# An encoder layer on one core: v's products ordered by the arrival of their weights, part of q moved behind v(1), block sums in x's old places, and some loads and splits issued sooner

## Chip, cores, metric

The kernel runs on one core of one Trainium2 chip. The metric is the device time of one execution in microseconds (us). The engines are called as in the profile: PE or TensorE (products), PEld (its weight loads), DVE or VectorE, ACT or ScalarE, POOL or GpSimd, SP (the queue that issues nearly all transfers).

## What is computed

One encoder layer on 1024 tokens of width 1024, in float32:

```python
h = layer_norm(x, emb_ln_g, emb_ln_b)
proj = h @ w_in                      # columns: q k v z_attn (512 each), u z_lru (512 each), g_attn g_lru (1024 each)
attn = neighbourhood_attention(q, k, v, rpb)       # 8 heads of 64, window 8 x 16 on a 16 x 64 grid
y_a  = attn * silu(z_a)
u    = centred_depthwise_conv(u, conv_w, conv_b)
y_b  = (rg_lru(u, ..., forward) + rg_lru(u, ..., backward)) * silu(z_b)
m    = sigmoid(g_a + b_merge[0]) * (y_a @ w_ba) + sigmoid(g_b + b_merge[1]) * (y_b @ w_bb)
out  = layer_norm(ALPHA * h + m @ w_out, ln_g, ln_b)
```

## The kernel before

The 1024 tokens are eight tiles of 128, i = 0 to 7. Every float32 operand of a product is split into a high and a low half that TensorE takes at full rate (ScalarE or POOL rounds the high half, `lo_of` subtracts it for the low one), and a product of two such operands is three products: high by high, low by high, high by low (`mm3`, the product at L131).

All five engines run in the order in which the code is written (`manual_schedule`), so an instruction that waits holds up what stands behind it in its engine's queue. The places in SBUF and PSUM are shared by tags; a tile waits for the last reader of what was there before.

The stages, in order:

- **Tiles, v and q** (lines 370 to 590). `load_x(i)` fetches a tile of x into one of five places (tag x). `ln_sums` takes mean and variance, `ln_v` (VectorE, tiles 0, 1, 3) or `ln_scale` and `ln_g` (ScalarE and POOL, the others) normalize it in place, `keep(i)` stores it for the end of the layer. `turn(i, kk)` transposes it on TensorE into a PSUM bank, four blocks of 128 columns in each half kk; `turn_hi` (ScalarE, L263) and `turn_lo` (VectorE) make the halves b_h and b_l of it. wv comes in four loads (`load_wv`) and is split by `wv_hi` (ScalarE, L186) and `wv_lo` (POOL). `v_part(i, kind, ks)` issues v's products of tile i (L308) for the weight blocks ks: kind h is b_h by wv's high half, a is b_l by the high half, w is b_h by the low half; 8 blocks each, 24 products in all. `q_part(m, n)` does the same for 128 columns m of q and k (m = 0 to 3) and 512 tokens n, with weights loaded by `qk_load` and split by `qk_prep` (ScalarE L169, POOL). The gains and offsets of the first layer norm are spread over the partitions by TensorE into four banks (gps) and copied to SBUF by `gb_copy`.
- **Block sums.** For tiles 4 to 7, `t_full` and `t_last` (L281 to L290) form sums of blocks of the transposed tile that the next stage multiplies, and `t_hi` and `t_lo` split them. t2 is written by `t_full` and overwritten by `t_last`.
- **Block stage.** 16 pairs of output columns, each by seven products of blocks (a11, a12, s2, s1, s3, s4, a22) in a loop over slots, for k, z, u and the gates; convolution and RG-LRU (`gate_stage`) run in the same slots. At slot `HEAD_AT` (109) and after it the first head's q, bias and k are fetched (`load_head`: `load_q`, `load_k`), and in `ending(2)` the second head's.
- **Attention.** Per head and tile: scores (L1036), bias and row minimum (L1046), exp (L1051), transposes (L1058), products with v (L1082). The merge of the LRU branch fills TensorE between them.
- **Late merge** (a loop over slots from L1253). `b_group` multiplies y_a with wb, `merge` applies the gate, adds the other branch and splits the sum; `b_split(0, j, A)` splits the weights of column block j, ScalarE the high half (L840), POOL the low one (L125). Of wb two blocks are held at a time.
- **Output** projection and layer norm, tile by tile; the last tile in pieces of 256 columns.

[...]

The order of the first products before the change:

```python
    for k in K0:
        v_part(0, "h", (k,))
        v_part(0, "a", (k,))
    v_part(0, "w", K0)
    v_part(0, "h", K1)
    v_part(0, "a", K1)
```

Of the kernel before, what the change touches and what calls it, by code (L numbers as in the profile page):

```python
# [67 lines left out]
def encoder_kernel(ctx, tc, x, gb1, gb, w_qk, w_v, w_s, w_ba, w_bb, w_gate, smalls, bias, w_out, out):  # L68
# [96 lines left out]

    def qk_prep(m):
        st = qk_s.pop(m)
        hi, lo = qk_w[m] = pair(wpl, [P, NK, P], f"wqk{m}", tag="w", bufs=2)
        A.copy(hi[:], st[:])  # L169
        lo_of(G, lo[:], st[:], hi[:])  # L170
# [3 lines left out]
    def load_x(i):  # L174
        xs[i] = ln.tile([P, D], F32, tag="x", bufs=5, name=f"x{i}")
        if i == 0:
            for c in range(2):
                SP.dma_start(xs[i][:, halves[c]], x[i][:, halves[c]])
        else:
            SP.dma_start(xs[i][:], x[i])  # L180
# [26 lines left out]
    def ln_sums(i):  # L207
        st, mv, e = (ln.tile([P, n], F32, tag=f"ln{n}{c}", bufs=2, name=f"ln{i}{c}")
                     for n, c in ((12, "t"), (2, "m"), (4, "e")))
        sts[i] = st, mv, e[:, 3:4], e[:, 0:3]  # L210
        sd, ve = sts[i][2:]
        for c in range(2):
            V.bn_stats(st[:, 6 * c:6 * c + 6], xs[i][:, halves[c]])
        V.bn_aggr(mv[:], st[:].rearrange("p (c s) -> p c s", c=2))
        A.activation(sd, mv[:, 1:2], AF.Sqrt, bias=eps_t[:])
        V.tensor_scalar(ve[:, 0:1], mv[:, 1:2], EPS, -0.5, ALU.add, ALU.mult)
# [59 lines left out]
    def t_full(i):  # L276

        for c, tag in ((1, "a21"), (2, "a12"), (3, "a22")):
            tt[i, c] = wsp.tile([P, 4, P], F32, tag=tag, bufs=2 if c == 3 else 1, name=f"t{c}_{i}")
        t1, t2, t3 = (tt[i, c][:] for c in (1, 2, 3))  # L280
# [6 lines left out]
    def t_last(i):  # L287
        t2 = tt[i, 4] = tt[i, 2]
        V.tensor_tensor(t2[:], f(B21[0], i), t2[:], ALU.subtract)
        V.tensor_tensor(t2[:], t2[:], f(B21[1], i), ALU.add)  # L290

    def t_hi(i, *cs):
        for c in cs:
            A.copy(Ts[c][0][:, :, ti(i)], tt[i, c][:])

    def t_lo(i, *cs):
        for c in cs:
            lo_of(G, Ts[c][1][:, :, ti(i)], tt[i, c][:], Ts[c][0][:, :, ti(i)])
# [28 lines left out]
    def q_part(m, n):  # L327
        o = qos[m, n] = bank(f"q{m}_{n}")
        run(mm3(o[:], [([t[:, 4 * kk + k, :] for t in qk_w[m]], [t[:, k, :] for t in blocks[kk][n]])
                       for kk in range(2) for k in range(4)]))  # L330
# [48 lines left out]
    load_wv(2)  # L379
    load_x(2)  # L380
    load_wv(3)
    SP.dma_start(sm[:], smalls)
    load_x(3)
    qk_load(0)
    load_x(4)
# [23 lines left out]
    turn_lo(0, 0)  # L409
    ln_sums(1)  # L410
    turn_lo(0, 1)
    for k in range(4, 8):
        wv_hi(k)
    for k in KS:
        wv_lo(k)
    for k in K0:
        v_part(0, "h", (k,))
        v_part(0, "a", (k,))
    v_part(0, "w", K0)
    v_part(0, "h", K1)  # L420
# [3 lines left out]
    keep(1)  # L424
    load_x(6)
    for kk in BOTH:
        turn(1, kk)
        turn_hi(1, kk)
    ln_sums(2)
    for z in BOTH:  # L430
        gb_copy(z, 0)
    ln_scale(2)
    for kk in BOTH:
        turn_lo(1, kk)
    for z in BOTH:
        gb_copy(z, 1)
    ln_g(2)
    ln_sums(3)
    v_part(1, "h", KS)
    v_part(0, "w", K1)  # L440
    v_part(1, "a", KS)
    qk_prep(0)
    v_hi(0)
    ln_v(3, 0)
    ln_v(3, 1)
    ln_sums(4)
    v_lo(0)
    psg.release()
    pst = tc.alloc_tile_pool(name="pst0", bufs=4, space=bass.MemoryType.PSUM, reuse_waits="tile")
    banks[0] = pst  # L450
# [4 lines left out]
    def tile_in(i, between=None, *args):  # L455

        for kk in BOTH:
            banks[0] = pst
            turn(i, kk)
            turn_hi(i, kk)  # L460
            banks[0] = ps0
            if kk == 0 and between:
                between(*args)
# [10 lines left out]
    banks[0] = ps0  # L474
    keep(2)
    keep(3)
    v_store(0)
    tile_in(2, v_part, 1, "w", KS)
    tile_in(3)
    tile_lo(2)  # L480
    ln_scale(4)
    ln_g(4)
    v_hi(1)
    tile_lo(3)
    qk_load(1)
# [4 lines left out]
    v_part(2, "h", KS)  # L490
    v_part(2, "a", KS)
    v_part(2, "w", KS)
    qk_prep(1)
# [3 lines left out]
    v_part(3, "h", KS)  # L497
    v_part(3, "w", KS)
# [6 lines left out]
    ln_next(7)  # L505
    t_full(4)
    v_part(3, "a", KS)
    t_hi(4, 2, 1, 3)
# [4 lines left out]
    q_part(0, 0)  # L513
    t_lo(4, 2, 1, 3)
    tile_in(5)
    q_hi(0, 0)
    tile_lo(5)
    t_last(4)
    q_lo(0, 0)
    q_store(0, 0)  # L520
    t_hi(4, 4)
    t_lo(4, 4)
# [6 lines left out]
    t_hi(5, 2, 1, 3)  # L529
    t_lo(5, 2, 1, 3)  # L530
    tile_in(6)
    tile_lo(6)
    t_last(5)
    t_hi(5, 4)
    t_lo(5, 4)
    for kind in "hwa":
        v_part(4, kind, KS)
    v_hi(4)
    v_lo(4)
    v_store(4)  # L540
    for kind in "hwa":
        v_part(5, kind, KS)
    tile_in(7)
    tile_lo(7)
    t_full(6)
    t_hi(6, 2, 1, 3)
    t_lo(6, 2, 1, 3)
    v_hi(5)
# [4 lines left out]
    t_lo(6, 4)  # L553
    for kind in "hwa":
        v_part(6, kind, KS)
    t_full(7)
    v_hi(6)
    v_lo(6)
# [336 lines left out]
    at(HEAD_AT, 1, lambda: load_k(0))  # L895
    at(HEAD_AT - 3, 1, head_start)
# [61 lines left out]
    def ending(k):  # L958
# [5 lines left out]
        if k == 2:  # L964
# [3 lines left out]
            load_head(1)  # L968
# [284 lines left out]
    for slot in range(2 * NK + 2):  # L1253
# [11 lines left out]
        if j < NK:  # L1265
# [179 lines left out]
```

## Time and profile before

| | |
|---|---|
| time, median of 3 runs | 683.49 us (683.47 to 684.93) |
| the profiled execution | 684.63 us, its span 682.8 us |
| granted TensorE clock, mean | 0.997 |
| TensorE busy | 665.8 us, 98% |
| VectorE, ScalarE, POOL busy | 72%, 53%, 52% |
| moved by DMA | 113.40 MB, mean 166 GB/s |

A row of the timeline is: start in us from the span's start, duration in us, engine, line of the kernel, operation, output <- inputs, shape, count, and in brackets the engine's idle time before it with what ended it. Rows that follow each other without a pause are merged (xN). A matmul's row ends with a modelled tail, so that rows overlap. SPq is SP's queue of issues. In the list of waits the numbers are: us in total, how often, the longest. Names are cut of their numbers: wv is v's weights, b_h and b_l the transposed tile's halves, ht the split block sums, tp a transpose in PSUM, ks and qs a head's k and q, wb the merge's weights, wo those of the output.

### The profile page before, as it was taken

Reading aid. Unit: us, or ns where it says so; the run is one execution under the profiler, and the core shown is the slowest. Engines: PE = TensorE matmul, PEld = TensorE weight load, DVE = VectorE, ACT = ScalarE, POOL = GpSimd, SP = SyncE. Lnnn points to the kernel's source line nnn. Section 1 sums busy time; section 2 is a strip of 40 time slices with the busy share of each in tenths; the row PEclk is TensorE's granted clock in tenths of the full one; section 3 lists DMA queues with packets and bytes.
Section 4 is the critical chain, followed back from the end, with each engine's and each line's share of the span. In section 5 each row is a group of like instructions: output and inputs, shape, how many; then the busy total and the mean of one; then the engine's idle time right before and its main releaser. Section 6 shows DMA issues by size and latency. Waiting matters only on the chain.

```text
span 682.8 us, 9299 instructions
## 1 busy us (share of the span) xinstructions
PE 665.8 (98%) x3177; PEld 554.4 (81%) x3177; DVE 494.7 (72%) x821; ACT 363.9 (53%) x612; POOL 353.8 (52%) x258
## 2 busy tenths in 40 slices
PE   7999999999999999999999999999999999999995
PEld 6787888888888888888788888788888878888884
DVE  7866766796899599879977785378787777533434
ACT  4544524247686677768576634467777554310110
POOL 5697461444576577567647544115355446435442
PEclk9999999999999999999999999999999999999998
DMA  8654165223324233431453557898794457512211
GB/s 327 227 187 154 63 231 171 78 92 124 124 92 145 71 108 123 170 124 48 170 199 112 182 176 253 305 353 308 250 327 144 176 197 271 189 62 93 92 62 61
DMA packets 48703, 113.40 MB, mean 166 GB/s; under 512 B 5057, under 2 KB 9745, under 8 KB 47121
## 3 DMA queue, kind: packets, MB, share of 16 engines
q1 hardware_dynamic: 48624, 112.81, 47.4%
q8 instruction: 25, 0.41, 0.2%
q14 instruction: 22, 0.17, 0.1%
q10 hardware_dynamic: 32, 0.01, 0.0%
HBM read 77.11 MB, written 35.68 MB: 165 GB/s over the span
## 4 chain that ended last, share of the span: by engine, by line
PE 80%; DVE 8%; DMA 4%; POOL 3%; issue 2%; ACT 1%; SPq 1%; DVEq 0%; POOLq 0%; ACTq 0%
PE a L131 29%; PE o L131 13%; PE s L131 11%; PE mb L131 10%; PE q L131 5%; PE acc L1082 3%; PE pt L1058 3%; PE s L1036 3%; POOL x L243 2%; PE v L308 2%; PE g L734 2%; DMA wvsl<-in_w_v_dram 1%; DMA ks<-k_d 1%; DMA wb<-in_w_ba_dram 1%; DVE ws_l L125 1%
## 5 line engine op out<-in xcount | busy, mean ns | idle before, releaser
L131 PE MATMUL o<-wo_h,ml 128*128 128x512 f32 (+1 forms) x136 | 51.2, 377 | 0.0
L131 PE MATMUL o<-wo_l,mh 128*128 128x512 f32 (+1 forms) x136 | 51.2, 376 | 0.0
L131 PE MATMUL o<-wo_h,mh 128*128 128x512 f32 (+1 forms) x136 | 51.2, 376 | 0.0
L1046 DVE CUSTOM_DVE_ANT_0 sc<-s,bias 128x384 f32<-128x384 f32 (+1 forms) x64 | 33.5, 523 | 22.9 <-PE s L1036 14.0
L131 PE MATMUL a<-ht_h,ws_h 128*128 128x512 f32 x128 | 49.9, 390 | 0.0
L131 PE MATMUL a<-ht_h,ws_l 128*128 128x512 f32 x128 | 49.8, 389 | 0.0
L131 PE MATMUL a<-ht_l,ws_h 128*128 128x512 f32 x128 | 49.8, 389 | 0.0
L131 PE MATMUL a<-b_h,wa_h 128*128 128x512 f32 x128 | 49.8, 389 | 0.0
L131 PE MATMUL a<-b_h,wa_l 128*128 128x512 f32 x128 | 49.8, 389 | 0.0
L131 PE MATMUL a<-b_l,wa_h 128*128 128x512 f32 x128 | 49.8, 389 | 0.0
L1335 DVE SCALAR_TENSOR_TENSOR z<-z,o 128x512 f32<-128x512 f32 (+1 forms) x17 | 11.2, 656 | 51.0 <-PE o L131 51.0
L1066 ACT CAST pt_h<-pt 128x384 fp32r<-128x384 f32 x64 | 29.0, 453 | 26.4 <-PE pt L1058 18.3
L1345 POOL TENSOR_TENSOR z<-z,gb 128x1024 f32<-128x1024 f32 x7 | 16.8, 2395 | 48.5 <-ACT z L1344 48.5
L1051 ACT ACTIVATE p<-sc,summ 128x384 f32<-128x384 f32 (+1 forms) x64 | 37.9, 592 | 5.2 <-DVE summ L1046 5.0
L1314 ACT ACTIVATE sd<-mv,eps_z 128x1 f32<-128x1 f32 x8 | 2.4, 294 | 67.1 <-DVE mv L1340 67.1
L308 PE MATMUL v<-wv,b_h 128*128 128x512 f32 x128 | 32.8, 399 | 2.7 <-ACT b_h L263 1.6
L125 DVE TENSOR_TENSOR pt_l<-pt,pt_h 128x384 fp32r<-128x384 f32 x64 | 33.2, 519 | 2.1 <-ACT pt_h L1066 1.6
L1036 PE MATMUL s<-ks,qs 128*128 128x384 f32 (+1 forms) x128 | 31.3, 326 | 1.1 <-DMA ks<-k_d 1.1
L308 PEld LDWEIGHTS v<-wv,b_h 128*128 128x128 f32 x128 | 23.6, 188 | 9.3 <-ACT b_h L263 2.3
L842 POOL CAST wb_h<-wb 128x512 fp32r<-128x512 f32 x9 | 7.0, 777 | 46.1 <-PE s L1036 18.3
L125 POOL TENSOR_TENSOR wb_l<-wb,wb_h 128x512 fp32r<-128x512 f32 x16 | 22.0, 1374 | 16.1 <-ACT wb_h L840 15.4
L1058 PEld LDWEIGHTS pt<-ident,p 128*128 128x128 f32 x176 | 23.1, 140 | 8.5
(438 smaller groups left out, 2199.8 us busy)
## 6 DMA issues: line engine op xcount, KB each, us to landing
ks<-k_d SPq DMA_DIRECT2D x8, 1024.0 KB, 8.0
h_d<-x SPq DMA_DIRECT2D x8, 512.0 KB, 4.4
v_d<-vs SPq DMA_DIRECT2D x8, 512.0 KB, 3.7
q_d<-q SPq DMA_DIRECT2D x8, 512.0 KB, 3.0
ga_d<-ga SPq DMA_DIRECT2D x16, 256.0 KB, 2.0
gb_d<-gb SPq DMA_DIRECT2D x16, 256.0 KB, 2.0
k_d<-k SPq DMA_DIRECT2D x8, 512.0 KB, 4.0
qs<-q_d SPq DMA_DIRECT2D x8, 512.0 KB, 3.9
```

Of the source, the lines that this page charges most:

```text
L125: eng.tensor_tensor(lo, full, hi.bitcast(F32), ALU.subtract)
L131: PE.matmul(o, a, b, start=first and i == 0, stop=last and i == len(prods) - 1, skip_group_check=not (first and last))
L243: G.tensor_tensor(z[:, halves[c]], z[:, halves[c]], gb_t[w][c][:], op)
L308: PE.matmul(vos[i][:], a, wv[kind == "w"][k][:], start=vn[i] == 0, stop=vn[i] == 23)
L734: PE.matmul(o[:, n, :], w[:, 2 * d + b, :], us[b][:, n * HALF:(n + 1) * HALF], start=z == 0, stop=z == 1)
L1036: PE.matmul(o[:, :P * len(near(t))], q[:, t * P:(t + 1) * P], k[:, z, keys], start=z == 0, stop=z == 1)
L1046: V.tensor_tensor_reduce(s[:, :w], o[:, :w], heads[h][2][:, b0:b0 + w], -1.0, 3.0e38, ALU.add, ALU.min, accum_out=sums[h][0][:, t:t + 1])
L1051: A.activation(probs[h % 2][t][:], scs.pop((h, t))[:, :w], AF.Exp, bias=sums[h][0][:, t:t + 1], scale=-1.0, accum_out=sums[h][1][:, t:t + 1])
L1058: PE.transpose(tp[:, n * P:(n + 1) * P], probs[h % 2][t][:, z * P:(z + 1) * P], ident[:])
L1066: A.copy(pt[0][:, span(b)], tps[h, b][:, :P * len(near(b))])
L1082: PE.matmul(acc[g][:, d:d + w], vvs[h // 2][:, b, h % 2, :], pt[:, a:a + w], start=b in (1, 6) and z == 0, stop=z == 1 and b == (4, 7)[g])
L1345: G.tensor_tensor(z[:], z[:], gb2[:, 0, :], ALU.mult)
```

## The change

Edits, in the order of the kernel:

- In the first stage the four banks of `ps0` get fixed places in a written order instead of the next free one.
- The loads: wv(3) goes ahead of x(2), wqk0 ahead of x(3), the small parameters behind x(4); wqk1 is issued ahead of x(6).
- The gains' copies are spread; wqk0's split stands right behind wv's, ahead of tile 1's b_h, and wqk1's ahead of tile 2's.
- v(0)'s products come as w0 w1, h4 h5, w2 w3, h6 h7 and so on; v(1) starts on the first half of tile 1. q(0,0) is issued in two parts of 256 tokens, the first behind v(1), the second behind v(3). The transposes of tiles 2 and 3 come in halves, those of tiles 6 and 7 one v earlier.
- The block sums t1, t2 and t4 take places of x that are free by then; t4 no longer overwrites t2.
- The second head's q, bias and k are issued right behind the first head's k.
- In the late merge, at slots 1 and 2, the split of the next weights stands ahead of the merge.

```diff
...
     hb12 = pool("hb12", "right")
 
     turns = []
+    places = itertools.chain((0, 1, 2, 3, 0, 1, 2, 0, 2, 3, 1), itertools.cycle((2, 3, 0, 1)))
 
     def bank(name):
         if turns:
             return banks[0].tile([P, HALF], F32, tag=next(turns[0]), bufs=2, name=name)
+        if banks[0] is ps0:
+            return ps0.tile([P, HALF], F32, tag=f"b{next(places)}", bufs=1, name=name)
         return banks[0].tile([P, HALF], F32, tag="bank", name=name)
...
         qk_s[m] = wpl.tile([P, NK, P], F32, tag="ws", bufs=1, name=f"wqk{m}_s")
         SP.dma_start(qk_s[m][:], w_qk[m])
 
+    def qk_hi(m):
+        qk_w[m] = pair(wpl, [P, NK, P], f"wqk{m}", tag="w", bufs=2)
+        A.copy(qk_w[m][0][:], qk_s[m][:])
+
+    def qk_lo(m):
+        hi, lo = qk_w[m]
+        lo_of(G, lo[:], qk_s.pop(m)[:], hi[:])
+
     def qk_prep(m):
-        st = qk_s.pop(m)
-        hi, lo = qk_w[m] = pair(wpl, [P, NK, P], f"wqk{m}", tag="w", bufs=2)
-        A.copy(hi[:], st[:])
-        lo_of(G, lo[:], st[:], hi[:])
+        qk_hi(m)
+        qk_lo(m)
 
     xs, sts = {}, {}
...
         xs[i] = ln.tile([P, D], F32, tag="x", bufs=5, name=f"x{i}")
         if i == 0:
-            for c in range(2):
-                SP.dma_start(xs[i][:, halves[c]], x[i][:, halves[c]])
+            for sl in halves:
+                SP.dma_start(xs[i][:, sl], x[i][:, sl])
         else:
...
     def gb_copy(z, c):
         A.copy(gb_t[z][c][:], gps[z][c][:])
 
-    def ln_sums(i):
+    def ln_stats(i):
         st, mv, e = (ln.tile([P, n], F32, tag=f"ln{n}{c}", bufs=2, name=f"ln{i}{c}")
...
         for c in range(2):
             V.bn_stats(st[:, 6 * c:6 * c + 6], xs[i][:, halves[c]])
         V.bn_aggr(mv[:], st[:].rearrange("p (c s) -> p c s", c=2))
+        V.tensor_scalar(ve[:, 0:1], mv[:, 1:2], EPS, -0.5, ALU.add, ALU.mult)
+
+    def ln_root(i):
+        st, mv, sd, ve = sts[i]
         A.activation(sd, mv[:, 1:2], AF.Sqrt, bias=eps_t[:])
-        V.tensor_scalar(ve[:, 0:1], mv[:, 1:2], EPS, -0.5, ALU.add, ALU.mult)
+
+    def ln_sums(i):
+        ln_stats(i)
+        ln_root(i)
 
...
 
     def t_full(i):
 
-        for c, tag in ((1, "a21"), (2, "a12"), (3, "a22")):
-            tt[i, c] = wsp.tile([P, 4, P], F32, tag=tag, bufs=2 if c == 3 else 1, name=f"t{c}_{i}")
-        t1, t2, t3 = (tt[i, c][:] for c in (1, 2, 3))
+        tt[i, 3] = wsp.tile([P, 4, P], F32, tag="a22", bufs=2, name=f"t3_{i}")[:]
+        t12 = ln.tile([P, 2, 4, P], F32, tag="x", bufs=5, name=f"t12_{i}")
+        tt[i, 1], tt[i, 2] = t12[:, 0], t12[:, 1]
+        if i in (4, 6):
+            tt["last"] = ln.tile([P, 2, 4, P], F32, tag="x", bufs=5, name=f"t4_{i}")
+        tt[i, 4] = tt["last"][:, i % 2]
+        t1, t2, t3 = (tt[i, c] for c in (1, 2, 3))
         A.copy(t3, tp4(i, 0))
...
         V.tensor_tensor(t3, tp4(i, 1), t3, ALU.subtract)
 
     def t_last(i):
-        t2 = tt[i, 4] = tt[i, 2]
-        V.tensor_tensor(t2[:], f(B21[0], i), t2[:], ALU.subtract)
-        V.tensor_tensor(t2[:], t2[:], f(B21[1], i), ALU.add)
+        t4 = tt[i, 4]
+        V.tensor_tensor(t4, f(B21[0], i), tt[i, 2], ALU.subtract)
+        V.tensor_tensor(t4, t4, f(B21[1], i), ALU.add)
 
     def t_hi(i, *cs):
         for c in cs:
-            A.copy(Ts[c][0][:, :, ti(i)], tt[i, c][:])
+            A.copy(Ts[c][0][:, :, ti(i)], tt[i, c])
 
     def t_lo(i, *cs):
         for c in cs:
-            lo_of(G, Ts[c][1][:, :, ti(i)], tt[i, c][:], Ts[c][0][:, :, ti(i)])
+            lo_of(G, Ts[c][1][:, :, ti(i)], tt[i, c], Ts[c][0][:, :, ti(i)])
 
...
 
     qos = {}
 
-    def q_part(m, n):
-        o = qos[m, n] = bank(f"q{m}_{n}")
-        run(mm3(o[:], [([t[:, 4 * kk + k, :] for t in qk_w[m]], [t[:, k, :] for t in blocks[kk][n]])
-                       for kk in range(2) for k in range(4)]))
+    def q_part(m, n, cols=slice(0, HALF)):
+        if (m, n) not in qos:
+            qos[m, n] = bank(f"q{m}_{n}")
+        run(mm3(qos[m, n][:, cols], [([t[:, 4 * kk + k, :] for t in qk_w[m]], [t[:, k, cols] for t in blocks[kk][n]])
+                                     for kk in range(2) for k in range(4)]))
 
...
     load_wv(1)
     load_x(1)
     load_wv(2)
+    load_wv(3)
     load_x(2)
-    load_wv(3)
+    qk_load(0)
+    load_x(3)
+    load_x(4)
     SP.dma_start(sm[:], smalls)
-    load_x(3)
-    qk_load(0)
-    load_x(4)
 
...
     wv_hi(3)
     turn_hi(0, 1)
     turn_lo(0, 0)
+    gb_copy(0, 0)
+    wv_hi(4)
+    wv_hi(5)
     ln_sums(1)
     turn_lo(0, 1)
-    for k in range(4, 8):
-        wv_hi(k)
+    wv_hi(6)
+    wv_hi(7)
+    gb_copy(1, 0)
     for k in KS:
         wv_lo(k)
+    qk_prep(0)
     for k in K0:
         v_part(0, "h", (k,))
         v_part(0, "a", (k,))
-    v_part(0, "w", K0)
-    v_part(0, "h", K1)
+    v_part(0, "w", (0, 1))
+    v_part(0, "h", (4, 5))
+    v_part(0, "w", (2, 3))
+    v_part(0, "h", (6, 7))
     v_part(0, "a", K1)
     ln_v(1, 0)
     ln_v(1, 1)
     keep(1)
+    qk_load(1)
     load_x(6)
-    for kk in BOTH:
-        turn(1, kk)
-        turn_hi(1, kk)
-    ln_sums(2)
-    for z in BOTH:
-        gb_copy(z, 0)
-    ln_scale(2)
-    for kk in BOTH:
-        turn_lo(1, kk)
+    turn(1, 0)
+    turn_hi(1, 0)
+    v_part(0, "w", (4, 5))
+    v_part(1, "h", K0)
+    turn(1, 1)
     for z in BOTH:
         gb_copy(z, 1)
+    turn_hi(1, 1)
+    v_part(0, "w", (6, 7))
+    ln_stats(2)
+    turn_lo(1, 0)
+    ln_root(2)
+    v_hi(0)
+    ln_scale(2)
+    turn_lo(1, 1)
     ln_g(2)
+    v_part(1, "w", K0)
+    v_part(1, "h", K1)
+    v_part(1, "a", KS)
+    v_part(1, "w", K1)
     ln_sums(3)
-    v_part(1, "h", KS)
-    v_part(0, "w", K1)
-    v_part(1, "a", KS)
-    qk_prep(0)
-    v_hi(0)
+    q_part(0, 0, slice(0, 256))
     ln_v(3, 0)
     ln_v(3, 1)
-    ln_sums(4)
-    v_lo(0)
+    v_hi(1)
+    qk_prep(1)
     psg.release()
     pst = tc.alloc_tile_pool(name="pst0", bufs=4, space=bass.MemoryType.PSUM, reuse_waits="tile")
-    banks[0] = pst
     for c, pl in zip((4, 3, 1, 2), hts):
         Ts[c] = pair(pl, [P, 4, HALF], f"ht{c}", tag=f"ht{c}")
     T1, T2, T3, T4 = (Ts[c] for c in (1, 2, 3, 4))
 
-    def tile_in(i, between=None, *args):
-
+    def turned_in(i, kk):
+        banks[0] = pst
+        turn(i, kk)
+        turn_hi(i, kk)
+        banks[0] = ps0
+
+    def tile_in(i):
         for kk in BOTH:
-            banks[0] = pst
-            turn(i, kk)
-            turn_hi(i, kk)
-            banks[0] = ps0
-            if kk == 0 and between:
-                between(*args)
+            turned_in(i, kk)
 
...
         ln_scale(i)
         ln_g(i)
 
-    banks[0] = ps0
     keep(2)
     keep(3)
+    turned_in(2, 0)
+    turned_in(3, 0)
+    ln_sums(4)
+    v_lo(0)
     v_store(0)
-    tile_in(2, v_part, 1, "w", KS)
-    tile_in(3)
-    tile_lo(2)
+    turned_in(2, 1)
+    turned_in(3, 1)
     ln_scale(4)
     ln_g(4)
-    v_hi(1)
+    tile_lo(2)
     tile_lo(3)
-    qk_load(1)
     v_lo(1)
     v_store(1)
     load_x(7)
     ln_next(5)
-    v_part(2, "h", KS)
-    v_part(2, "a", KS)
-    v_part(2, "w", KS)
-    qk_prep(1)
+    for kind in "hwa":
+        v_part(2, kind, KS)
     keep(4)
     ln_next(6)
     v_hi(2)
-    v_part(3, "h", KS)
-    v_part(3, "w", KS)
+    for kind in "hw":
+        v_part(3, kind, KS)
     v_lo(2)
...
     tile_in(4)
     tile_lo(4)
     ln_next(7)
+    v_part(3, "a", KS)
     t_full(4)
-    v_part(3, "a", KS)
-    t_hi(4, 2, 1, 3)
     v_hi(3)
     v_lo(3)
     v_store(3)
     keep(6)
-    q_part(0, 0)
-    t_lo(4, 2, 1, 3)
+    q_part(0, 0, slice(256, HALF))
+    t_last(4)
     tile_in(5)
     q_hi(0, 0)
+    t_hi(4, 2, 1, 3, 4)
+    t_lo(4, 2, 1, 3, 4)
     tile_lo(5)
-    t_last(4)
     q_lo(0, 0)
     q_store(0, 0)
-    t_hi(4, 4)
-    t_lo(4, 4)
     keep(7)
     q_part(1, 0)
...
     q_lo(1, 0)
     q_store(1, 0)
-    t_hi(5, 2, 1, 3)
-    t_lo(5, 2, 1, 3)
-    tile_in(6)
-    tile_lo(6)
     t_last(5)
-    t_hi(5, 4)
-    t_lo(5, 4)
     for kind in "hwa":
         v_part(4, kind, KS)
+    tile_in(6)
     v_hi(4)
+    t_hi(5, 2, 1, 3, 4)
+    t_lo(5, 2, 1, 3, 4)
+    tile_lo(6)
     v_lo(4)
     v_store(4)
+    t_full(6)
     for kind in "hwa":
         v_part(5, kind, KS)
     tile_in(7)
-    tile_lo(7)
-    t_full(6)
+    v_hi(5)
     t_hi(6, 2, 1, 3)
     t_lo(6, 2, 1, 3)
-    v_hi(5)
+    tile_lo(7)
     v_lo(5)
     v_store(5)
...
     t_hi(6, 4)
     t_lo(6, 4)
+    t_full(7)
     for kind in "hwa":
         v_part(6, kind, KS)
-    t_full(7)
     v_hi(6)
+    t_last(7)
     v_lo(6)
...
                 qk_prep(m + 2)
                 if m == 0:
                     qk_load(3)
-                    t_hi(7, 2, 1, 3)
-                    t_lo(7, 2, 1, 3)
-                    t_last(7)
-                    t_hi(7, 4)
-                    t_lo(7, 4)
+                    t_hi(7, 2, 1, 3, 4)
+                    t_lo(7, 2, 1, 3, 4)
                     s_load(0, "a21", "a22", "a12")
...
         at(slot + 3, 0, lambda t=t: yb_lo(t))
     at(HEAD_AT, 1, head_pool)
     at(HEAD_AT, 1, lambda: load_k(0))
+    at(HEAD_AT, 1, lambda: load_head(1))
     at(HEAD_AT - 3, 1, head_start)
...
             b_load(1, 2)
             for n in range(2):
                 g_load(1, 1, n)
-            load_head(1)
         if k < 2:
...
             run(b_group(0, j, n, ya, o, range(3 if slot < 2 else 4)))
             if 0 < slot < 3:
                 run(b_group(0, 0, slot - 1, ya, sums_m[slot - 1], range(3, 4)))
-                merge(0, slot - 1, sums_m[slot - 1])
             if n == 0 and j > 0:
                 b_split(0, j + 1, A)
+            if 0 < slot < 3:
+                merge(0, slot - 1, sums_m[slot - 1])
```

## Prediction

> **What bounds the kernel now.** I read the page's head, then TensorE's own list of waits, then TensorE's timeline, and last the other engines around each hole.
>
> ```profile
> span 682.8 us, 9299 instructions
> PE 665.8 (98%) x3177; PEld 554.4 (81%) x3177; DVE 494.7 (72%) x821; ACT 363.9 (53%) x612; POOL 353.8 (52%) x258
> PE v L308 <- ACT b_h L263: 1.6, 3, 0.9
> PE s L1036 <- DMA ks<-k_d: 1.1, 1, 1.1
> PE mb L131 <- POOL wb_l L125: 0.9, 1, 0.9
> PE mb L131 <- ACT wb_h L840: 0.5, 1, 0.5
> ```
>
> TensorE is busy for 98% of the span, so the change can't lift the bound; it can only close holes. The list names three places: v's first products, the second head's keys, and the weights (wb) of the last merge. The change touches all three.
>
> **Before 38 us.** First a ledger of TensorE from v's first product to tile 4's transposes:
>
> ```profile
> 9.88 0.50 PE L308 MATMUL v<-wv,b_h 128*128 128x512 f32 x1
> 28.70 2.11 PE L308 MATMUL v<-wv,b_h 128*128 128x512 f32 x8 [0.49 <-ACT b_h L263]
> 32.46 5.61 PE L308 MATMUL v<-wv,b_h 128*128 128x512 f32 x24
> 37.90 1.03 PE L254 MATMUL tp<-ident,x 128*128 128x128 f32 x8
> 38.69 2.10 PE L308 MATMUL v<-wv,b_l 128*128 128x512 f32 x8
> ```
>
> 24 products take 37.90 - 32.46 = 5.44 us, 0.227 each; 8 transposes take 38.69 - 37.90 = 0.79. Between 9.88 and 37.90 lie 28.0 us with 88 products (20.0; v(0) to v(2) and two thirds of v(3)) and 24 transposes (2.4): 5.6 us are holes, nearly all before 28.7.
>
> The change moves wv(3)'s load ahead of x(2)'s, orders v(0)'s products by the arrival of weights, lets v(1) begin on half a tile, splits wqk0 behind the last of wv, and issues q(0,0) for its first 256 tokens behind v(1): 24 half-width products. Their price stands in the last tile of the output projection, where 24 steps lie between these two starts:
>
> ```profile
> 671.72 0.28 PE L131 MATMUL o<-wo_l,mh 128*128 128x256 f32 x1
> 674.60 0.28 PE L131 MATMUL o<-wo_l,mh 128*128 128x256 f32 x1
> ```
>
> That is 2.88 us, 0.120 each. Half of a full-width pass costs 2.72, so the split adds 0.16 per half. Whether the half fits the holes is decided by those who supply TensorE:
>
> ```profile
> 8.91 5.02 POOL L125 TENSOR_TENSOR wv<-wvsh,wv 128x512 fp32r<-128x512 f32 x4 [7.60 <-ACT wv L186]
> 13.88 5.01 POOL L125 TENSOR_TENSOR wv<-wvsl,wv 128x512 fp32r<-128x512 f32 x4
> 10.78 1.29 DVE L213 BATCH_NORM_STATS2 ln1t<-x 128x6 f32<-128x512 f32 x2 [0.23 <-DMA x<-in_x_dram]
> 14.65 1.14 ACT L186 CAST wv<-wvsl 128x512 fp32r<-128x512 f32 x2 [0.98 <-DMA wvsl<-in_w_v_dram]
> 14.42 0.75 DVE L230 SCALAR_TENSOR_TENSOR x<-x,ln1e,gps 128x512 f32<-128x512 f32 x1
> 17.75 1.07 ACT L263 CAST b_h<-tp 128x512 fp32r<-128x512 f32 x2 [1.95 <-PE tp L254]
> 22.89 1.03 ACT L169 CAST wqk_h<-wqk_s 128x1024 fp32r<-128x1024 f32 x1
> 21.37 5.25 POOL L243 TENSOR_TENSOR x<-x,gb 128x512 f32<-128x512 f32 x4 [2.48 <-ACT x L237]
> 26.59 2.35 POOL L125 TENSOR_TENSOR wqk_l<-wqk_s,wqk_h 128x1024 fp32r<-128x1024 f32 x1
> ```
>
> POOL makes one low half of wv each 1.25 us, the last at 18.9, in either order. From x(1)'s landing (10.78) to wv(3)'s (14.65) three loads of 512 KB arrive, 1.29 each. In the new order wv(3) lands near 13.4, x(2) near 14.7, wqk0 near 15.9.
>
> Walked through, in the new order: h4 and h5 fill the time until w3's low half is made (13.9); v(0)'s a products end at 15.7; tile 1's first transposes follow at once, its first half being ready at 14.42 + 0.75 = 15.2. Now ScalarE is late: wqk0's cast (15.9 to 16.9) stands in its queue ahead of tile 1's b_h (0.54, to 17.5), and behind that wait v(1) h and VectorE's b_l. After w4, w5 (to 16.65) TensorE waits 0.9. w6, w7 and v(1) then run to 23.9, q's half to 26.8. Tile 2's square root now stands behind tile 1's second b_h on ScalarE, so POOL starts x(2)'s gains at 22.35 instead of 21.37 and ends them at 27.6: a hole of 0.5 before x(2)'s second half is turned. wqk1's load goes out when POOL frees its place (18.9 + 2.35 = 21.3), lands behind x(5) and h(1) near 26.5, and its cast delays b_h of tiles 2 and 3: a hole of 0.2 in v(2) h. POOL does wqk1's low part between tiles 2 and 4, so tile 4 is ready near 36.7. I arrive at tile 4's transposes at 37.85, where it was 37.90, with half of q(0,0) done: a gain of 2.7. Bounds: 1.0 if wqk0 and wqk1 land one load (1.3) late less what holes remain behind them; 4.2 if the 0.9, 0.5 and 0.2 close too.
>
> At no cost: wqk1's issue ahead of x(6), which waits for h(1)'s store anyway; the gains' copies, two of 0.5 put into ScalarE's wait for wv (0.98 in the row at 14.65). If that wait is gone they cost 0.5.
>
> **38 to 77 us.**
>
> ```profile
> 64.19 1.19 PE L254 MATMUL tp<-ident,x 128*128 128x128 f32 x8
> 66.24 3.96 PE L308 MATMUL v<-wv,b_h 128*128 128x512 f32 x16 [0.86 <-ACT b_h L263]
> 47.83 0.69 DVE L282 TENSOR_TENSOR t<-tp,b_h 128x512 f32<-128x512 f32 x1 [1.83 <-ACT t L281]
> 48.56 0.93 DVE L283 TENSOR_TENSOR t<-t,b_l 128x512 f32<-128x512 f32 x1
> 50.13 0.68 DVE L285 TENSOR_TENSOR t<-tp,t 128x512 f32<-128x512 f32 x1
> 52.42 0.69 DVE L125 TENSOR_TENSOR vs<-v,vs 128x512 fp32r<-128x512 f32 x1 [1.61 <-ACT vs L315]
> 53.03 1.28 DVE L125 TENSOR_TENSOR b_l<-tp,b_h 128x512 fp32r<-128x512 f32 x2
> 57.16 1.77 DVE L289 TENSOR_TENSOR t<-b_h,t 128x512 f32<-128x512 f32 x1 [2.85 <-POOL ht_l L125]
> 58.96 1.66 DVE L290 TENSOR_TENSOR t<-t,b_l 128x512 f32<-128x512 f32 x1
> 69.09 0.69 DVE L290 TENSOR_TENSOR t<-t,b_l 128x512 f32<-128x512 f32 x1
> ```
>
> Before, v(6) starts 2.05 after tile 7's transposes, which need 0.79; ScalarE's queue is late with b_h. Now tiles 6 and 7 are turned one v ahead, which leaves b_h 5.4 us. Gain 1.2, less 0.16 for q's second half (the first's is inside the 2.7). With t4 in a place of its own L289 no longer waits 2.85 for POOL.
>
> Late next is VectorE's chain. From 47.83: t_full(4) 3.0, v's low 0.7, t_last(4) 3.4, b_l(5) 1.3, q's low 0.7, t_full(5) 3.0, q's low 0.7, t_last(5) 2.4 (between the two lengths of L290), b_l(6) 1.3, end 64.3. TensorE wants b_l(6) at 37.85 + transposes of four tiles 3.2, v(3) a 1.8, q's half 2.9, then q(1,0), v(4), v(5) 16.3, and 16 products of v(6) 3.6: 65.7. Slack 1.4, no stall in the sum; bounds 0 and 2.
>
> L290 takes 0.69 in one row and 1.66, beside a POOL pass, in another. [...]
>
> **Second head.**
>
> ```profile
> 422.37 0.55 SPq L864 DMA_DIRECT2D ks<-k_d  x1
> 434.73 1.87 SPq L864 DMA_DIRECT2D ks<-k_d  x1
> 443.65 0.47 PE L1036 MATMUL s<-ks,qs 128*128 128x256 f32 x2 [1.07 <-DMA ks<-k_d]
> ```
>
> Head 1's keys went out 12.4 us after head 0's and landed 1.07 too late; now they go right behind them, near 424. Gain 1.1. Its 2 MB now stand in SP's queue ahead of the last gates' stores and the next merge's first loads (g, wb), at 1.29 per 512 KB some 5 us. g(1,0,0) then lands about a microsecond after VectorE wants it, which nobody on TensorE waits for. Bounds: 0 (landing no sooner) and 1.2.
>
> **Late merge.**
>
> ```profile
> 550.11 1.05 ACT L1280 CAST wo_h<-wos 128x1024 fp32r<-128x1024 f32 x1
> 552.79 0.62 ACT L840 CAST wb_h<-wb 128x512 fp32r<-128x512 f32 x1
> 553.46 0.50 PE L131 MATMUL mb<-ya_h,wb_h 128*128 128x512 f32 x1 [0.50 <-ACT wb_h L840]
> 553.49 1.28 POOL L125 TENSOR_TENSOR wb_l<-wb,wb_h 128x512 fp32r<-128x512 f32 x1 [7.76 <-ACT wb_h L840]
> 554.82 0.50 PE L131 MATMUL mb<-ya_h,wb_l 128*128 128x512 f32 x1 [0.86 <-POOL wb_l L125]
> ```
>
> The holes are 0.5 with a busy tail of 0.16, and 1.36 - 0.23 = 1.13 between the two products: 1.8. wb_h waited in ScalarE's queue behind the merge's cast. Put ahead of it, it starts at 551.2, wb_l ends near 553.2; TensorE wants wb_h at 552.8, wb_l at 553.0. Gain 1.5 (bounds 0.8, with POOL's pass held up by VectorE, and 1.8). The merge's own cast waits for VectorE, not for ScalarE.
>
> **Sum.** 2.7 + 1.2 - 0.16 + 1.1 + 1.5 = 6.3, and 0.05 from 37.90 to 37.85: 6.4. The profiled execution took 684.63 (1.8 around its span of 682.8) and would take 678.2; the runs' median, 683.49, goes to **677.1**. A measurement of this kernel can't tell less than 0.2% (1.4 us) from no change. The forecast's own range is 675.7 (1.4 of the holes left before 38 us closed) to 678.6 (1.5 of the 6.4 lost).
>
> **Rivals.**
> A. The hole moves to ScalarE: wqk0's and wqk1's casts wait for their transfers with b_h behind them. For it: the 0.9 already in my walk. Against: 1.29 per load is steady. Price 1.8, a load and a half: 678.9. Chance 0.15.
> B. VectorE's chain sets v(6) and v(7): t3 has one place until v(7) is done, so its copy on ScalarE waits for POOL, with b_h(7) behind it. For it: a slack of 1.4 only. Price 2, the bound above: 679.1. Chance 0.12.
> C. Head 1's loads help nothing, since SP or the transfers are full: 1.1 lost, 678.2. Chance 0.06.
> A and B together, with their stalls doubled, come within 0.2% (over 682.1): chance 0.03.
> [...] Chance 0.06, other mishaps included.
>
> **How the numbers follow.** The forecast has 0.58, A 0.15, B 0.12, C 0.06: faster 0.91; same 0.03; slower 0.06. The range 675.5 to 680.2 holds the forecast, C, and most of A and B; it leaves out A with B, D, and the case that all bounds are reached (4.2 + 1.2 - 0.16 + 1.2 + 1.8 = 8.2, 675.3).
>
> **What would show it.** Right: tile 4's transposes near 37.9 behind 24 half-width q products; no wait before v(6); the first product after v(7) near 73.4; no ks wait on TensorE; wb waits under 0.4. Wrong: v(1) h later than 18.5 with wqk0's cast in front (A); v(6) or v(7) released by b_h or b_l (B, D); keys still landing after the first scores of head 1 (C).

## The result, and the profile after

The changed kernel takes 678.42 us (median of six runs, 677.68 to 678.67); the kernel before, beside it, 683.48 (683.09 to 684.93). The ratio of the means is 0.9919 [0.9906, 0.9931] (in brackets, here and below, the 95% interval). The forecast was 677.1, range 675.5 to 680.2. The profiled execution took 678.46 us, its span 676.7; 678.2 was forecast for it. In the runs beside the experiments the kernel before took 684.5 to 684.7 and the changed one 678.88, a ratio of 0.9911 [0.9898, 0.9924].

The head of the page of after, and two rows of its list of TensorE's waits:

```profile
span 676.7 us, 9344 instructions
PE 665.2 (98%) x3201; PEld 555.7 (82%) x3201; DVE 492.7 (73%) x821; ACT 364.5 (54%) x612; POOL 355.8 (53%) x258
PE v L328 <- ACT b_h L279: 0.5, 1, 0.5
PE mb L134 <- DVE ya_l L128: 0.3, 1, 0.3
```

TensorE's busy time hardly moved (665.8, now 665.2); of the 6.1 us that the span lost, 5.5 came out of its holes. The waits for the second head's keys and for wb are gone from the list. In before v waited three times for b_h and once each for POOL's wv, ScalarE's wv and b_l; now it waits once, for b_h.

The timeline of after up to tile 4's transposes, ScalarE's and POOL's rows first, then TensorE's:

```profile
15.37 1.05 ACT L171 CAST wqk_h<-wqk_s 128x1024 fp32r<-128x1024 f32 x1 [0.93 <-DMA wqk_s<-in_w_qk_dram]
16.32 0.58 ACT L279 CAST b_h<-tp 128x512 fp32r<-128x512 f32 x1
21.76 5.29 POOL L259 TENSOR_TENSOR x<-x,gb 128x512 f32<-128x512 f32 x4 [2.15 <-ACT x L253]
16.95 1.19 PE L328 MATMUL v<-wv,b_h 128*128 128x512 f32 x4 [0.53 <-ACT b_h L279]
17.98 0.60 PE L270 MATMUL tp<-ident,x 128*128 128x128 f32 x4
26.32 1.91 PE L270 MATMUL tp<-ident,x 128*128 128x128 f32 x16
27.98 3.96 PE L328 MATMUL v<-wv,b_h 128*128 128x512 f32 x16
37.23 1.03 PE L270 MATMUL tp<-ident,x 128*128 128x128 f32 x8
```

The order of the walk is seen: wqk0's cast waits for its transfer, tile 1's b_h stands behind it, v(1) h waits for that, at 16.95. POOL's gains end at 27.05, and no hole stands ahead of the 16 transposes of tiles 2 and 3, since q's half runs until 26.3. Tile 4's transposes start at 37.23 (37.85 forecast).

From tile 5 to v(7) in after, TensorE, VectorE, ScalarE:

```profile
61.00 1.03 PE L270 MATMUL tp<-ident,x 128*128 128x128 f32 x8
61.79 3.89 PE L328 MATMUL v<-wv,b_h 128*128 128x512 f32 x16
65.51 1.98 PE L328 MATMUL v<-wv,b_l 128*128 128x512 f32 x8
47.07 1.79 DVE L303 TENSOR_TENSOR t<-t,b_l 128x512 f32<-128x512 f32 x1
57.83 0.69 DVE L302 TENSOR_TENSOR t<-tp,b_h 128x512 f32<-128x512 f32 x1 [2.51 <-ACT t L301]
58.55 0.69 DVE L303 TENSOR_TENSOR t<-t,b_l 128x512 f32<-128x512 f32 x1
61.08 1.45 DVE L309 TENSOR_TENSOR t<-b_h,t 128x512 f32<-128x512 f32 x1
62.56 1.67 DVE L310 TENSOR_TENSOR t<-t,b_l 128x512 f32<-128x512 f32 x1
64.15 1.27 DVE L128 TENSOR_TENSOR b_l<-tp,b_h 128x512 fp32r<-128x512 f32 x2
57.21 0.59 ACT L301 COPY t<-tp 128x512 f32<-128x512 f32 x1 [3.03 <-POOL ht_l L128]
```

v(6) follows the transposes at once, and the first product after v(7) starts at 72.77 (73.4 forecast). But tile 6's two low halves end at 64.15 + 1.27 = 65.42, and TensorE takes the first of them at 65.51: 0.1 us between, where the forecast had 1.4.

In the last merge of after, and POOL's gate in before (the last row):

```profile
546.61 0.62 ACT L865 CAST wb_h<-wb 128x512 fp32r<-128x512 f32 x1
547.31 1.30 POOL L128 TENSOR_TENSOR wb_l<-wb,wb_h 128x512 fp32r<-128x512 f32 x1 [6.03 <-ACT wb_h L865]
541.88 0.50 PE L134 MATMUL mb<-ya_l,wb_h 128*128 128x512 f32 x1 [0.31 <-DVE ya_l L128]
537.04 2.54 POOL L1145 TENSOR_TENSOR za<-za,rsb 128x512 f32<-128x512 f32 x2 [9.54 <-DMA rsb<-rs_d]
541.47 2.54 POOL L1120 TENSOR_TENSOR za<-za,rsb 128x512 f32<-128x512 f32 x2 [8.68 <-DMA rsb<-rs_d]
```

The waits for wb are gone. This profile has a short one for ya_l in their place, which follows the last row sums (rsb) on their way back from memory: POOL's gate starts 0.52 after the merge's first product (536.52), in before (541.47) 0.27 ahead of it (541.74). Counted from start to start, 0.23 is lost ahead of ya_h and 0.48 ahead of ya_l.

### The profile page after: what moved, and what is told of

Its sections match the earlier page's. It is cut to its first block, busy times and chain, and to the rows that moved or that the text cites. A ratio compares the mean times of both kernels' runs of the same rounds, so it can differ in the third digit from the quotient of the medians.

```text
span 676.7 us, 9344 instructions
## 1 busy us (share of the span) xinstructions
PE 665.2 (98%) x3201; PEld 555.7 (82%) x3201; DVE 492.7 (73%) x821; ACT 364.5 (54%) x612; POOL 355.8 (53%) x258
## 4 chain that ended last, share of the span: by engine, by line
PE 89%; DVE 6%; DMA 2%; issue 1%; SPq 1%; ACT 0%; POOL 0%; DVEq 0%; POOLq 0%
PE a L134 30%; PE o L134 13%; PE mb L134 12%; PE s L134 11%; PE q L134 6%; PE v L328 6%; PE acc L1107 3%; PE s L1061 3%; PE pt L1083 3%; PE g L759 2%; DMA wqk_s<-in_w_qk_dram 2%; DVE ws_l L128 1%; PE tp L270 1%; DMA rsb<-rs_d 1%; DVE uc L717 1%
## 5 line engine op out<-in xcount | busy, mean ns | idle before, releaser
L1083 PE MATMUL pt<-ident,p 128*128 128x128 f32 x176 | 29.6, 272 | 0.0
```

The source lines that it names most:

```text
L1083: PE.transpose(tp[:, n * P:(n + 1) * P], probs[h % 2][t][:, z * P:(z + 1) * P], ident[:])
```

## The experiments

Theory: four parts, each with its own hole (first stage, v(6), keys, late merge). Rivals: the terms depend on each other or on something else in the change. All ratios are to the kernel before, run beside them. A place "from v(1)" is counted from the 25th of v's products in time, which leaves the loads at the start out. In the changed kernel this is v(1)'s third product, 0.58 us after its first, since two weight blocks of v(0) come later; the expectations below call it v(1)'s start.

**The kernel before again** (`b_again`, no edit).

> The kernel before, unchanged, once more. Its runs so far lie in two groups, 683.1 to 683.5 and 684.93, and the profiled execution of before, from which every term of the forecast was read, belongs to the upper one. Theory: one of the holes before 38 us is longer in the upper group, by about 1.3 us, so that the forecast's 2.7 for that stretch was read from too slow an execution. Rival: the 1.3 us lies elsewhere (start of the kernel, the second head's keys, the last merge). A second profile tells which holes keep their lengths: keys 1.23, last merge 0.66 and 1.13, v(6) 1.15 in the first profile. Time: median 683.5, ratio 1.000.

684.37, ratio 1.000 [0.9991, 1.0009]. Of the holes, v(6) (1.15) and the last merge (0.62 and 1.13) kept their lengths; that of the keys was 0.62 in place of 1.23, and POOL's gate stood as before. No hole before 38 us moved by 1.3: that guess is wrong. The 62 runs of before beside the experiments lie between 682.98 and 686.16, without two groups. What differs between the profiles is mainly when transfers land: the first loads (x(1) 0.66 us apart in the two profiles of the changed kernel), the keys (with the old load 7.3 to 9.7 after their issue), the last row sums (POOL's gate starts 3.5 to 4.5 after the issue of their read).

**Only the second head's loads sooner** (`b_head`).

```diff
+    at(HEAD_AT, 1, lambda: load_head(1))
...
-            load_head(1)
```

> The kernel before with one edit: the second head's queries, bias and keys are loaded right behind the first head's keys. Theory (the forecast's 1.1 for the keys): the hole of 1.23 us ahead of head 1's first scores goes, time 682.4 (gain 1.0 to 1.2). Rival: the transfers ahead of it are already full, or the last gates and the next merge's loads come late in its place: the hole goes but another of a similar size opens, time 683.5.

683.32, ratio 0.9984 [0.9976, 0.9993]: 1.2 us. The wait for ks is not in its list, and no new one is.

**Only the late merge's order** (`b_merge`).

```diff
-                merge(0, slot - 1, sums_m[slot - 1])
             if n == 0 and j > 0:
                 b_split(0, j + 1, A)
+            if 0 < slot < 3:
+                merge(0, slot - 1, sums_m[slot - 1])
```

> The kernel before with one edit: in the last merge the next weight block is split ahead of the merge's own cast on ScalarE. Forecast's term: both holes of 0.66 and 1.13 us between the products of the second block close, gain 1.5, time 682.0. Rival, after the comparison of the two profiles: the holes close but the merge then waits about 0.7 us more for the attention's last low half (ya_l) at its start, as in the profile of after, gain 0.9 to 1.1, time 682.5. If that wait is not in this run's profile, it hangs on the last row sums' transfer of the one execution and not on the edit.

682.48, ratio 0.9971 [0.996, 0.9983]: 2.0 us, six runs. In its profile the merge takes 1.5 less (45.63 to 44.12 from its first product to the output projection's), with one hole of 0.21 ahead of ya_l. The interval reaches from 1.2 to 2.7 us, so the two agree.

**Only tile 6's b_h ahead of tile 5's sums on ScalarE** (`b_turn6`).

```diff
+    tile_in(6)
     t_hi(5, 2, 1, 3)
     t_lo(5, 2, 1, 3)
-    tile_in(6)
     tile_lo(6)
```

> The kernel before with one edit: the casts of tile 6's transposed halves (b_h) stand ahead of the three casts of tile 5's block sums in ScalarE's queue. t4 keeps its old place (it overwrites t2). Theory: the 1.15 us ahead of v(6) came from ScalarE's order alone, gain 1.0 to 1.15, time 682.4, b_h of tile 6 at about 62.2 us of the profile in place of 65.6. Rival: it came from VectorE's chain with t4 written over t2, which this kernel keeps: then b_l of tile 6 or another wait opens before v(6)'s or v(7)'s products and the gain is under 0.4, time over 683.1.

684.4, ratio 1.0001 [0.9992, 1.001]. TensorE's rows:

```profile
64.51 1.16 PE L254 MATMUL tp<-ident,x 128*128 128x128 f32 x8
65.43 3.91 PE L308 MATMUL v<-wv,b_h 128*128 128x512 f32 x16
71.51 1.89 PE L308 MATMUL v<-wv,b_h 128*128 128x512 f32 x7 [0.36 <-ACT b_h L263]
```

v(6) waits no more, but v(7) does (0.52 from start to start): ScalarE is held by t_last's sum (its cast at 69.86 waited 3.87 for it), so tile 7's b_h is late too (70.87). The rival was right: the order alone is worth 0.5 in the profile and nothing that the time shows.

**The same, and t4 in a place of its own** (`b_turn6_t4`).

```diff
...
-        t2 = tt[i, 4] = tt[i, 2]
+        if i in (4, 6):
+            tt["last"] = ln.tile([P, 2, 4, P], F32, tag="x", bufs=5, name=f"t4_{i}")
+        t4 = tt[i, 4] = tt["last"][:, i % 2]
...
```

> The kernel before with two edits: tile 6's b_h ahead of tile 5's block sums on ScalarE (alone it closed the 1.0 us ahead of v(6) and opened 0.52 ahead of v(7)), and t4 in a place of its own in x's old places, so that t_last no longer waits 2.85 us for POOL to read t2. Theory: the second wait came from VectorE's and ScalarE's chain through t4 over t2, so the 0.52 goes too: v(6) and v(7) without a wait, first product behind v(7) 1.0 to 1.15 sooner than in before counted from tile 4's transposes, time 0.5 below the run with the first edit alone. [...]

683.38, ratio 0.9981 [0.9972, 0.9989]: 1.1 us. Both waits are gone:

```profile
64.86 3.89 PE L310 MATMUL v<-wv,b_h 128*128 128x512 f32 x16
68.58 1.98 PE L310 MATMUL v<-wv,b_l 128*128 128x512 f32 x8
70.39 3.82 PE L310 MATMUL v<-wv,b_h 128*128 128x512 f32 x16
```

From tile 4's transposes to v(7)'s last product lie 37.85 us, in before 39.16: 1.3. So the cast's order needed t4 off t2 to pay. What t4's place is worth without the new order was not run.

**Only the part before tile 4** (`a_first38`; block sums, head loads and merge as in before).

> Only the part of the change before tile 4 (load order, v(0)'s and v(1)'s products, wqk0 behind wv, q(0,0) in two halves); block sums and their order from tile 4 on, the second head's loads and the last merge as in before. Forecast's terms: 2.7 less 0.16, time 682.0 beside a before of 684.5. By the profile of after (3.4 less 0.16, since the holes of 0.5 and 0.2 that the forecast allowed for did not appear): 681.3. Rival: VectorE's old chain, now wanted 3.2 earlier by TensorE, takes part of it back ahead of v(6), over 682.3.

683.58, ratio 0.9982 [0.997, 0.9994]: 1.1, less than any forecast for it. Its profile has the gain: from v's first product to v(7)'s last 2.95 us less than in before, after 0.58 lost between tile 6's transposes, which wait for t_full(5), and 0.37 ahead of v(6) (the rival). In this execution most of it is then given back at two transfers:

```profile
PE s L1063 <- DMA ks<-k_d: 2.0, 1, 2.0
PE mb L134 <- ACT ya_h L1163: 0.4, 1, 0.4
```

The keys landed 9.7 us after their issue (7.3 to 8.8 in the five other kernels with the old load), the last row sums 0.77 after the merge's start. Counted from start to start, 1.07 is lost at the merge's start, with the old order of the merge. Whether most of its executions lose that much there is open, and so is what the first stage alone is worth in the time: its twelve runs lie between 681.91 and 686.80. The four parts alone (first stage, v(6), keys, merge) multiply to 0.9982 x 0.9981 x 0.9984 x 0.9971 = 0.9918, against 0.9911 for the whole; each factor is known to about 0.001, so that no dependence between the parts is seen, and a small one is not ruled out.

**The changed kernel again** (`a_again`).

> The changed kernel once more, as the measure for the other runs beside it, and a second profile. If the 0.23 and 0.48 us at the last merge's start in its first profile belong to one slow transfer, they are under 0.3 here, and the merge takes 43.9 to 44.3 us up to the output projection in place of 44.69. Time 678.4 to 679.0.

678.88. The merge took 44.59, with 0.48 ahead of ya_l, so the first expectation fails. In the seven profiles of kernels with the new order of the merge (`a_k3_late`, which moves products too, left out), between 0 and 0.71 was lost at its start, in six of them something. With the old order it was 0 in both profiles of before, 0.09 in `b_head`, 0.12 in `b_turn6`, 0.47 in `b_turn6_t4` and 1.07 in `a_first38`. So the wait is not brought by the new order. It goes with the trip of the row sums, counted from the issue of their read to the start of POOL's gate: trips of up to 3.73 us lost 0.26 at most, trips of 3.79 to 4.47 lost 0.47 to 1.07. Tile 4's transposes start at 37.92 here, v(1) 0.68 later than in the first profile, since x(1) landed 0.66 later: from v(1) both took 19.7.

**q(0,0) whole** (`a_qwhole`; the written order of the banks is fitted to it).

```diff
...
-    q_part(0, 0, slice(0, 256))
...
-    q_part(0, 0, slice(256, HALF))
+    q_part(0, 0)
```

> The changed kernel with one part undone: q(0,0) in one piece behind v(3), nothing of it behind v(1). Forecast's account: the half fills time in which TensorE would otherwise wait for tile 2's gains on POOL, so tile 4's transposes come at the same time (37.2) and the whole half is lost: +2.7 less 0.16 for the split, time after + 2.6. Rival: the gain of the first stage came from the load order and v(0)'s product order, and the half only pushes v(2) back: then tile 4's transposes come 2.7 earlier and the time stays within 0.4 of after.

683.24, ratio 0.9975 [0.9964, 0.9987]: 4.4 over the changed kernel, more than theory and rival said. The transposes of tiles 2 and 3 and two windows of its profile:

```profile
25.39 0.66 PE L270 MATMUL tp<-ident,x 128*128 128x128 f32 x4 [0.84 <-POOL x L259]
27.13 2.82 PE L270 MATMUL tp<-ident,x 128*128 128x128 f32 x12 [1.09 <-DVE x L246]
24.00:27.00 3.00, 1.20 (x7) 0.54 (x5) 2.86 (x8) 0.58 (x1) 2.86 (x3) 0.99 0.74 305
27.00:30.00 3.00, 2.87 (x13) 2.75 (x14) 2.67 (x8) 2.69 (x6) 2.52 (x2) 0.50 0.91 333
```

(Columns of the windows: window and its length, TensorE, its loads, VectorE, ScalarE, POOL busy, granted clock, share of DMA, GB/s.) TensorE had two holes of 1.0 and 1.25 us, waiting for POOL's gains and for tile 3 on VectorE; then its granted clock was 0.50, and 12 transposes took 2.47 us, 0.21 each in place of 0.107. So tile 4's transposes come 20.7 after v(1), 1.0 later than with the half, and the half is still to do (2.5 up to v(7)'s last product). Another 1.15 opened at 126.15: ScalarE's load of its table (1.28 us, row at 112.90) came behind a wait of 1.77 for VectorE in this build, in after (106.73) behind none, which sent VectorE's next chain off 1.3 late. That is a side effect of the edit. The three come to 4.65.

**The same, with zeros in the half's place** (`a_qwhole_busy`).

```diff
...
-    q_part(0, 0, slice(0, 256))
+    dummy = bank("dummy")
+    for _ in range(40):
+        PE.matmul(dummy[:, :P], zero[:], zero[:], start=True, stop=True)
...
-    q_part(0, 0, slice(256, HALF))
+    q_part(0, 0)
```

> The changed kernel with q(0,0) in one piece behind v(3), and in its first half's place behind v(1) 40 products of zeros into a bank that nobody reads, about 2.2 us of work for TensorE at the full clock. Theory: in the run with nothing in that place TensorE stood idle for 2.2 us of 3, its granted clock fell to 0.50 until 30 us, and the transposes of tiles 2 and 3 took 0.214 each in place of 0.107: with the zeros the clock stays at 1.00 and tile 4's transposes come 19.7 to 19.9 us after v(1)'s start (20.7 without them, 19.7 in the changed kernel). Rival: they come late because the gains or the transposes' inputs are late: 20.5 or more.

682.34, ratio 0.9961 [0.9948, 0.9974].

```profile
24.00:27.00 3.00, 3.00 (x46) 2.73 (x43) 2.93 (x6) 1.05 (x2) 2.92 (x3) 1.00 0.70 264
27.00:30.00 3.00, 2.79 (x18) 2.19 (x17) 2.79 (x10) 2.93 (x7) 2.68 (x2) 1.00 0.91 356
```

The clock stays at 1.00 and tile 4's transposes come 19.7 after v(1), as with the half. The hole at the table load is in this run too, so 3.5 over the changed kernel remain, near the 2.5 of the half and that 1.15. So the half of q costs nothing where it stands, and beside its own 2.5 us it keeps the clock at 1.00, where without it and without the zeros it was 0.50.

**wqk0's cast behind tile 1's b_h** (`a_bh_first`).

```diff
-    qk_prep(0)
...
     turn_hi(1, 0)
+    qk_prep(0)
```

> The changed kernel with wqk0's cast and low part issued behind the cast of tile 1's first transposed half (b_h) on ScalarE. Theory (forecast's 0.9 and rival A, seen as 0.70 us ahead of v(1) h): the hole at 16.0 closes to under 0.15 and tile 4's transposes come 0.5 to 0.65 sooner, time after - 0.6. Rival: q's half ends sooner but tile 2's gains on POOL do not, so a hole of about 0.45 opens ahead of tile 2's second half and the gain is 0.2 or less.

678.33, ratio 0.9908 [0.9894, 0.9921]. The hole of 0.70 shrank to 0.38 and another of 0.23 opened inside v(1). From tile 1's first transposes to tile 4's lie 21.8 us, in the changed kernel 21.9: 0.1 gained. The rival was right on the size, not on the place: the new hole is inside v(1), not ahead of tile 2's second half.

**Products of the last head pair later** (`a_k3_late`).

```diff
-            run(b_group(0, j, n, ya, o, range(3 if slot < 2 else 4)))
-            if 0 < slot < 3:
-                run(b_group(0, 0, slot - 1, ya, sums_m[slot - 1], range(3, 4)))
+            run(b_group(0, j, n, ya, o, range(3 if slot < 3 else 4)))
+            if slot == 2:
+                for q in BOTH:
+                    run(b_group(0, 0, q, ya, sums_m[q], range(3, 4)))
+                run(b_group(0, j, n, ya, o, range(3, 4)))
...
```

> The changed kernel with the last merge's first two groups finished later: the products that need the last head pair (k = 3 of groups 0 and 1) stand behind three quarters of group 2, and the two merges of their results move with them. Theory: in the changed kernel the merge starts before the last row sums are back from memory, so the 0.23 and 0.48 us ahead of ya_h and ya_l are its regular price; they close, time after - 0.5 (0.2 may come back as a wait for wb_l, which ends 0.2 late for group 2). Rival: they belong to one slow transfer of the profiled execution (the kernel before with the merge edit alone showed 0.21), and nothing is to be gained: within 0.2 of after.

678.19, ratio 0.9904 [0.9891, 0.9918]. ya_h and ya_l are waited for no more, but wb_l is, 0.52: the hole changed its cause. No version beat the changed kernel by more than the measurement can tell.

**One VectorE pass more** (`a_extra`).

```diff
-        V.tensor_tensor(t4, f(B21[0], i), tt[i, 2], ALU.subtract)
+        for _ in range(2 if i == 5 else 1):
+            V.tensor_tensor(t4, f(B21[0], i), tt[i, 2], ALU.subtract)
```

> The changed kernel with one VectorE pass more: the first pass of tile 5's t_last (two inputs in SBUF, 1.45 us in the profile of after) is done twice, with the same result, ahead of tile 6's low halves. The forecast gave VectorE's chain a slack of 1.4 us ahead of v(6)'s last eight products; by that, the time stays within 0.1. By the profile of after the low halves end 0.1 before they are wanted: then v(6) waits 1.0 to 1.4 for b_l and the time is 1.0 to 1.4 over the changed kernel's.

679.6 beside 678.88, five and four runs that overlap; the clear answer is in the profile:

```profile
61.55 3.89 PE L329 MATMUL v<-wv,b_h 128*128 128x512 f32 x16
66.33 2.11 PE L329 MATMUL v<-wv,b_l 128*128 128x512 f32 x8 [0.89 <-DVE b_l L128]
60.82 3.15 DVE L310 TENSOR_TENSOR t<-b_h,t 128x512 f32<-128x512 f32 x2
```

v(6)'s low products, 3.72 after its start in after, come 4.78 after it. The pass added 1.7 (3.15 for two, 1.45 for one), and 1.06 of it reached v(6), 1.2 v(7)'s last product (from v(1)). So the slack was 0.6, not 1.4. It is more than the 0.1 between the ends because the first of the two low halves is enough to go on. In after that one ends at 64.84, 0.7 ahead of 65.51; here it ends at 66.28, and the products start at 66.33.

## Why the prediction was right, step by step

**Before 38 us: 2.7 forecast.** Half of q was done by tile 4's transposes, which came at 37.23 and 37.92 in two executions (37.85 forecast, 37.90 in before). With 2.72 for the half that is a gain of 3.4 and 2.7. The 0.9 ahead of v(1) was 0.70, at its place; with wqk0's cast behind b_h 0.38 of it stayed and 0.23 came up inside v(1). The 0.2 in v(2) did not come. Nor did the 0.5 ahead of tile 2's second half, and here the walk had a step wrong: in the changed order the first half of tile 3 is turned in between. Eight transposes, 0.87 us from 26.32, carry TensorE over the 0.73 until POOL's gains end at 27.05; in the walk's own numbers, 26.8 and 27.6, they would have closed the hole too. The half-width products cost what was said (24 of them from 23.45 to 26.32, 2.87). That the clock falls without them (to 0.50 in `a_qwhole`), for another 1.0, was not foreseen. It is no part of the gain over before, where the clock stayed at 1.00.

**38 to 77: 1.2.** Measured 1.3 with both edits. The place of the gain was right, its cause was told wrongly: no transposes were moved one v ahead (the section on the change says so too). Tile 6's stand ahead of v(5), in before ahead of v(4); tile 7's stay ahead of v(6). What moved is the cast of b_h ahead of the sums on ScalarE, and that pays only with t4 off t2.

**VectorE's chain: slack 1.4 forecast; 0.1 by the same reckoning, 0.6 by the experiment.** The first half of rival B's mechanism came: ScalarE's copy for t3 waited 3.03 for POOL (row at 57.21), and VectorE 2.51 for it. The second half, a stall of v(6) or v(7), did not. From 46.35 to 65.42 the chain took 19.1 us where the forecast had 16.5; 2.5 of the difference is that wait, and the passes themselves differ by 0.1 in sum. The chain also began 1.5 sooner than the row of before from which it was counted (47.83), and TensorE wanted its result 0.2 sooner than forecast: 1.4 - 2.6 + 1.5 - 0.2 is the 0.1 that was left. Single passes with two SBUF inputs were mis-sized both ways: t_full(4)'s (row at 47.07) took 1.79 where 0.93 was taken, t_last(4) 2.7 for 3.4, t_last(5) 3.1 for 2.4. Beside POOL such passes took 1.12 to 1.79 in after, without it 0.69 (row at 58.55). Why a pass is longer beside POOL the runs do not show. Nor does any show the slower case, D, to which the forecast gave 0.06: the highest ratio of the experiments is 1.0001 (`b_turn6`), and the longest such pass in after took 1.79. B's chance of 0.12 was low for a mechanism that was half there and whose stall was missed by 0.6.

**Keys: 1.1.** Alone 1.2. The hole in before was 1.23 in one profile and 0.62 in the other; the forecast was read from the longer one.

**Late merge: 1.5.** Alone 1.5 in the profile, 2.0 in the time; in the changed kernel 0.93 and 1.04, because 0.71 and 0.57 were lost at the merge's start in these two executions, waiting for the row sums. POOL's pass on wb, which the forecast's lower bound of 0.8 has held up by VectorE, took 1.30 in after (row at 547.31), 1.28 in before: such a hold-up was not shown. The forecast left the wait for the row sums out: it looked at VectorE and at the weights, not at the row sums' way through memory. The runs show it with the old order too (section on `a_again`); both profiles of before happened to have none.

**The sum.** 6.4 forecast against 6.17 between the two profiled executions, 5.8 in the runs beside the experiments and 5.1 between the medians of the first six. That it came so near is in part luck. Up to v(7)'s last product, counted from v's first, the change gained 4.6 and 4.0 in its two profiles where 3.8 was forecast; the merge gave 0.6 and 0.5 less than forecast; and 0.3 was lost in the block stage, for which nothing was forecast. There, from v(7)'s last product to the first scores, every kernel with the new first stage takes 359.0 to 359.1 us (360.3 and 360.4 with q whole, with the hole of 1.15) and those without it 358.7 to 358.8; the cause was not found. **The time itself** was 1.3 too low by one step: "the runs' median, 683.49, goes to 677.1". Three runs were too few for it; the profiled 684.63 was close to the typical time (684.5), and 678.2 the better forecast.

## What to carry to other kernels

A hole of TensorE is closed by useful work only if that work's inputs are there already; its worth is then more than its own time where it keeps the granted clock up (here 2.5 us of its own and 1.0 more, with the clock at 1.00 in place of 0.50). A cast that is late in an in-order queue can hide a second one behind it (here, with the wait of v(6) gone in `b_turn6`, 0.52 ahead of v(7)): follow the same queue one tile further before counting the gain. And when a chain on another engine is costed, count the waits inside it (here 2.5 us for a copy that stood behind POOL) and not its passes alone, and look at what is left of the slack, not only at whether there is a stall.

## What was not expected of the hardware

In `a_qwhole` the granted clock fell to 0.50 at 27.0 us and came back about 3.4 us later (0.50 from 27.0 to 30.0, 0.87 on average from 30.0 to 31.5). Ahead of it lay a stretch of 3 us in which TensorE was busy for 1.20, the longest single pause being 1.25 us. Counted without the four transposes in that stretch, the pause ahead of the fall was 2.6 us (from the last product of v(1), over at 24.4, to 27.0). In before, the holes between 22.8 and 28.7 us add up to 1.9, with eight products of v in between, and the clock stayed at 1.00. What length of pause or share of idle time brings the fall no run here tells.

From the issue of the last row sums' read to the start of POOL's gate 3.5 to 4.5 us passed in the 14 profiles, and x(1) landed 0.66 us apart in the two profiles of the changed kernel. This is as much as single edits of this change are worth.
